# One 512-column product for two of 256, a ring of four banks for it, and a first stage fed by a transposed input

## The chip, the cores and the metric

The program runs on one core of a Trainium2 chip. The metric is the time of one execution on the device in microseconds (us). Engines are named as in the profile: PE is TensorE (PEld its loads of the stationary operand), DVE is VectorE, ACT is ScalarE, POOL is GpSimd, SP is SyncE, which issues the DMAs.

## The reference

Two layers over x of 256 tokens by 1024 features, all float32. Each layer is FFN, mixer, FFN; layer 0 mixes with a causal convolution, layer 1 with a gated recurrence (HGRN2). Every sub-layer normalizes its input and its output. Cut to what the change touches:

```python
def rms_norm(x, gain):
    y = x * lax.rsqrt(jnp.mean(x * x, axis=-1, keepdims=True) + EPS)
    return y * gain

def swiglu_ffn(x, w_in, w_out):                       # w_in 1024 x 5632, w_out 2816 x 1024
    gate, up = jnp.split(x @ w_in, 2, axis=-1)
    return (jax.nn.silu(gate) * up) @ w_out

for layer in range(2):
    h = swiglu_ffn(rms_norm(x, g[0]), ffn_w_in[layer, 0], ffn_w_out[layer, 0])
    x = x + 0.5 * rms_norm(h, g[1])
    x = x + rms_norm(mixer(rms_norm(x, g[2])), g[3])  # convolution or HGRN2
    h = swiglu_ffn(rms_norm(x, g[4]), ffn_w_in[layer, 1], ffn_w_out[layer, 1])
    x = x + 0.5 * rms_norm(h, g[5])
```

## The kernel before

Precision comes from splitting. Each float32 operand becomes a rounded high part and the rest (`split`: an ACT cast, then a DVE subtract), and each product is three products: high by high, high by low, low by high. Weights stream from HBM in pieces of 128 x 1024 (`weight`: one DMA of 512 KB from SP's queue into one of four `raw` buffers, then the split into one of ten `wh` and ten `wl` buffers). A chunk of an FFN is 256 hidden features: four pieces of the first matrix and two of the second; there are 11 chunks.

An FFN begins with `start`. For each of the two blocks of 128 tokens `pre_norm` transposes x by PE (8 transposes, two PSUM banks of the ring `tr`) and evacuates it with the gain, high part by ACT, low part by DVE, into `xth` and `xtl`; the row's mean square and its power of -0.5 (by POOL) follow beside it and are applied later as a scale of each token. For the first chunk `project` (in the very first FFN `project_both`) multiplies with the tokens as stationary operand and 512 columns of weights moving; `up` applies the scale and the gate, `turn` transposes the result. For the chunks 1 to 10 `up_both` computes both blocks at once with the hidden features as output rows: `channels` has the weights as stationary operand, and the 256 tokens move. It does two parts, the gate's rows and the up rows, each of 8 x 3 products of 256 columns into one half of an `mm` bank, and one DVE multiply of 512 columns (L286) takes both out of PSUM with the tokens' scales. Then come a sigmoid, two multiplies and a split. `down` multiplies chunk c-1 with the second matrix (`expand`, 512 columns) into two accumulator banks for each block. `post_norm` ends a sub-layer. The second block's end (`rest`) is run within the next sub-layer's `start`. HGRN uses `channels` eight times too, for its forget gates and queries.

PSUM has eight banks: four for the ring `acc` (the four accumulators of an FFN), two for `mm`, two for `tr`.

The text of the kernel is in program order. A planner puts the instructions of each engine in order by their readiness and priority; `tc.issue_after(ins)` pins what is traced in its block behind `ins` on that engine's queue. Before, the first weights' splits are pinned behind the first evacuations in this way. DMAs go through SP's queue in order; a weight's DMA waits there until its `raw` buffer is free.

The start: x is loaded in three DMAs, then the weights; PE transposes block 0, starts the projection, transposes block 1, and goes on.

Of the kernel before, what the change touches and what calls it, by code (L numbers as in the profile page):

```python
# [8 lines left out]
F32 = mybir.dt.float32  # L9
F32R = mybir.dt.float32r  # L10
# [30 lines left out]
def trunk_kernel(  # L41
    ctx: ExitStack,
    tc: tile.TileContext,
    x_in: bass.AP,
    wts: bass.AP,
# [28 lines left out]
    def narrow(tag, dtype=F32):  # L74
        return new(sb, [P, 256], dtype, tag, {"e": 4, "hid": 4}[tag])
# [7 lines left out]
    def mm():  # L83
        return new(ps, [P, 512], F32, "mm", 2)

    def tr():
        return new(ps, [P, 512], F32, "tr", 2)
# [11 lines left out]
    xth = const.tile([P, NT * D], F32R, name="xth")  # L99
    xtl = const.tile([P, NT * D], F32R, name="xtl")  # L100
    xkh = xth.rearrange("p (t k m) -> p k t m", t=NT, m=P)
    xkl = xtl.rearrange("p (t k m) -> p k t m", t=NT, m=P)
    gcol = const.tile([P, G_END], F32, name="gcol")
    nc.sync.dma_start(xs[0][:, :512], x_in[0, :P, :512])
    nc.sync.dma_start(gcol, cols)
    nc.sync.dma_start(xs[0][:, 512:], x_in[0, :P, 512:])
    nc.sync.dma_start(xs[1], x_in[0, P:, :])

    stream = [0]
    ahead = []  # L110
    last_hi = [None]
    last_split = [None]
    last_raw = [None]

    def weight(fine=False):
        n, half = divmod(stream[0], 2)
        stream[0] += 1
        src = new(sb, [P, 1024], F32, "raw", 4)
        last_raw[0] = nc.sync.dma_start(src, wts[n, :, half * 1024 : half * 1024 + 1024]).ins
# [3 lines left out]
        with ExitStack() as held:  # L123
            if stream[0] <= 4:
                held.enter_context(tc.issue_after(last_hi[0]))
            for a in range(0, 1024, step):
                split(hi[:, a : a + step], lo[:, a : a + step], src[:, a : a + step])
        return hi, lo

    def split(dst_h, dst_l, src):  # L130
        last_split[0] = act.copy(dst_h, src).ins  # L131
        dve.tensor_tensor(dst_l, src, dst_h.bitcast(F32), op=ALU.subtract)  # L132
# [28 lines left out]
    def pre_norm(t, gi):  # L161
        src = xs[t]
        hi, lo = xth[:, t * D : (t + 1) * D], xtl[:, t * D : (t + 1) * D]
        for h in range(2):
# [4 lines left out]
            for j in range(4):  # L169
                k = h * 4 + j  # L170
                g = gcol[:, gi * KD + k : gi * KD + k + 1]
                last_hi[0] = act.activation(hi[:, k * P : (k + 1) * P],
                                            pt[:, j * P : (j + 1) * P], AF.Copy, scale=g).ins
# [8 lines left out]
        if gi == 0:  # L182
            return hi, lo, None
        return hi, lo, mean_square(src)

# [35 lines left out]

    def project_both(xt, ws):
        o = [mm(), mm()]
# [619 lines left out]
```

## Time and profile before

| | |
|---|---|
| median of three timed runs | 1033.92 us (1032.2 to 1036.58) |
| the profiled execution's own time | 1030.74 us |
| its span | 1029.0 us |
| granted TensorE clock, mean | 0.996 |
| bytes moved by DMA | 181.14 MB, mean 176 GB/s |
| PE, PEld, DVE, ACT busy | 98%, 89%, 69%, 49% of the span |

All rows come from the profiled execution. Busy time is the time in which an engine had at least one instruction under way. Matmuls overlap, so a matmul's listed duration is longer than the time that it adds to a stream; the step from one start to the next shows the latter.

### The profile page before, as it was taken

The numbers are of one execution on the slowest core, as the hardware profiler recorded it, in microseconds if no ns is written. First come the engines' busy times: TensorE is split into PE (matmuls) and PEld (weight loads), VectorE is DVE, ScalarE is ACT, GpSimd is POOL, SyncE is SP. The second block draws the span as 40 slices with busy tenths as digits, with TensorE's granted clock in tenths as the row PEclk, the third lists the DMA queues.
The fourth block names the chain that finished last, engine by engine and source line by source line (L and its number), as shares of the span: only waits on it lengthen the run. The fifth ranks groups of instructions, "written<-read, shape, count | busy, mean of one in ns | idle before, by whom it ended". The sixth has DMA issues, their size and how long they took to land. (4 is left out here: it accounts for less than half of the span.)

```text
span 1029.0 us, 16850 instructions
## 1 busy us (share of the span) xinstructions
PE 1004.7 (98%) x6676; PEld 913.2 (89%) x6676; DVE 705.6 (69%) x1092; ACT 504.7 (49%) x852; POOL 71.0 (7%) x116
## 2 busy tenths in 40 slices
PE   7999999999899999999999999999999999999997
PEld 6999999888779999998899999989888879999996
DVE  6766666899887565658675656677676586666663
ACT  7544444764485444446544444574143473444441
POOL 1000000000010000000100000021343020000000
PEclk9999999999999999999999999999999999999999
DMA  7756464843536465647464646555222555564641
GB/s 254 259 198 212 156 211 142 270 164 111 182 101 226 168 199 170 223 152 241 144 206 163 205 164 226 185 202 179 87 84 91 176 175 186 161 215 155 215 143 41
DMA packets 50510, 181.14 MB, mean 176 GB/s; under 512 B 5985, under 2 KB 6113, under 8 KB 50432
## 3 DMA queue, kind: packets, MB, share of 16 engines
q1 hardware_dynamic: 50432, 180.07, 52.6%
q8 instruction: 52, 0.85, 0.3%
q14 instruction: 26, 0.21, 0.1%
HBM read 179.00 MB, written 1.05 MB: 175 GB/s over the span
## 5 line engine op out<-in xcount | busy, mean ns | idle before, releaser
L132 DVE TENSOR_TENSOR wl<-raw,wh 128x1024 fp32r<-128x1024 f32 (+1 forms) x386 | 400.6, 1059 | 200.4 <-ACT wh L131 196.8
L131 ACT CAST wh<-raw 128x1024 fp32r<-128x1024 f32 (+1 forms) x386 | 336.5, 923 | 275.4 <-PE mm L282 127.5
L281 PE MATMUL mm<-xth,wh 128*128 128x256 f32 x1408 | 396.3, 281 | 0.0
L282 PE MATMUL mm<-xtl,wh 128*128 128x256 f32 x1408 | 396.3, 281 | 0.0
L283 PE MATMUL mm<-xth,wl 128*128 128x256 f32 x1408 | 396.0, 281 | 0.0
L281 PEld LDWEIGHTS mm<-xth,wh 128*128 128x128 f32 x1408 | 265.8, 189 | 3.2 <-DVE e L335 0.7
L282 PEld LDWEIGHTS mm<-xtl,wh 128*128 128x128 f32 x1408 | 265.1, 188 | 2.6
L283 PEld LDWEIGHTS mm<-xth,wl 128*128 128x128 f32 x1408 | 266.1, 189 | 0.5 <-DVE wl L132 0.2
L136 PE MATMUL acc<-wl,b 128*128 128x512 f32 x352 | 137.8, 391 | 0.0
L137 PE MATMUL acc<-wh,b 128*128 128x512 f32 x352 | 137.7, 391 | 0.0
L135 PE MATMUL acc<-wh,b 128*128 128x512 f32 x352 | 137.6, 391 | 0.0
L137 PEld LDWEIGHTS acc<-wh,b 128*128 128x128 f32 x352 | 66.1, 188 | 14.1
L135 PEld LDWEIGHTS acc<-wh,b 128*128 128x128 f32 x352 | 66.1, 188 | 11.5
L136 PEld LDWEIGHTS acc<-wl,b 128*128 128x128 f32 x352 | 66.1, 188 | 11.4
L334 ACT ACTIVATE e<-ga 128x256 f32<-128x256 f32 x80 | 33.4, 418 | 79.8 <-DVE ga L286 79.8
L242 PE MATMUL mm<-wh,xth 128*128 128x512 f32 x176 | 70.7, 401 | 0.0
L243 PE MATMUL mm<-wl,xth 128*128 128x512 f32 x176 | 70.1, 398 | 0.0
L286 DVE TENSOR_TENSOR ga<-mm,scales 128x512 f32<-128x512 f32 x88 | 60.2, 685 | 12.4 <-PE mm L283 12.2
L146 POOL TENSOR_SCALAR tiny<-tiny 128x1 f32<-128x1 f32 (+1 forms) x30 | 8.4, 281 | 802.6 <-ACT b L212 711.5
L131 ACT CAST b<-e 128x256 fp32r<-128x256 f32 x80 | 32.4, 405 | 53.2 <-DVE e L336 53.2
L246 PE MATMUL mm<-wh,xtl 128*128 128x512 f32 x176 | 49.8, 397 | 0.0
L132 DVE TENSOR_TENSOR b<-e,b 128x256 fp32r<-128x256 f32 x80 | 33.8, 422 | 21.3 <-ACT b L131 21.3
(156 smaller groups left out, 877.4 us busy)
## 6 DMA issues: line engine op xcount, KB each, us to landing
raw<-wts SPq DMA_DIRECT2D x328, 512.0 KB, 5.0
b<-rows SPq DMA_DIRECT2D x10, 512.0 KB, 6.1
out_dram<-x SPq DMA_DIRECT2D x4, 256.0 KB, 2.1
x<-x_in SPq DMA_DIRECT2D x2, 256.0 KB, 2.8
x<-x_in SPq DMA_DIRECT2D x1, 512.0 KB, 4.2
b<-dft SPq DMA_DIRECT2D x1, 371.0 KB, 4.6
ca<-masks SPq DMA_DIRECT2D x1, 192.0 KB, 4.8
b<-w_dw SPq DMA_DIRECT2D x1, 124.0 KB
```

The lines of the kernel that those rows point to most:

```text
L131: last_split[0] = act.copy(dst_h, src).ins
L132: dve.tensor_tensor(dst_l, src, dst_h.bitcast(F32), op=ALU.subtract)
L135: pe.matmul(o, lh, rh, start=first, stop=False)
L136: pe.matmul(o, lh, rl, start=False, stop=False)
L137: pe.matmul(o, ll, rh, start=False, stop=last)
L242: pe.matmul(o, hi[:, kp], wh[:, sl], start=k == 0, stop=False)
L243: pe.matmul(o, hi[:, kp], wl[:, sl], start=False, stop=False)
L246: pe.matmul(o, a, w, start=False, stop=h == 1 and n == 3)
L281: pe.matmul(og, wh[:, cs], xkh[:, k], start=k == 0, stop=False)
L282: pe.matmul(og, wh[:, cs], xkl[:, k], start=False, stop=False)
L283: pe.matmul(og, wl[:, cs], xkh[:, k], start=False, stop=k == KD - 1)
L286: dve.tensor_tensor(pair(res), pair(o), scales.unsqueeze(1).broadcast_to([P, 2, SEQ]), op=ALU.mult)
```

## The change

- `channels`: for each k one product of 512 columns, weight high part by (x high, x low), and one of 256, weight low part by x high. Each part has a bank of its own: the first half collects high by high and low by high, the second half high by low. ACT copies the second half to SBUF, DVE adds it to the first, and a DVE multiply within SBUF applies the scales. For the moving operand high and low parts of x stand in one tile `xt` (block, part, k, token), with two small unused tiles on both sides of it that shift its address.
- PSUM: `mm` has four banks, and `tr` takes banks of `acc`'s four.
- The start: x is also handed over transposed, in four pieces of 256 features by 256 tokens. `boot` replaces `pre_norm` and `project_both` in the first FFN: for each piece it scales it into `xt`, loads and splits one weight, multiplies block 0, squares the piece, and multiplies block 1; the mean squares come from four small products with a column of ones. The order is pinned on ACT, DVE, PE and SP (`behind`). Twelve products of the identity with itself run before. The weights of chunk 1 are loaded before the second matrix's of chunk 0. The gains' DMA moves to ACT's queue.
- The plain x is loaded in chunk 4 of the first FFN, for the residual.
- The taps of the convolution get a row of zeros, and the ring `e` has six buffers where it had four.

```diff
@@ rings
-        return new(sb, [P, 256], dtype, tag, {"e": 4, "hid": 4}[tag])
+        return new(sb, [P, 256], dtype, tag, {"e": 6, "hid": 4}[tag])
-        return new(ps, [P, 512], F32, "mm", 2)
-
-    def tr():
-        return new(ps, [P, 512], F32, "tr", 2)
+        return new(ps, [P, 512], F32, "mm", 4)
+
+    tr = acc
...
-    xth = const.tile([P, NT * D], F32R, name="xth")
-    xtl = const.tile([P, NT * D], F32R, name="xtl")
-    xkh = xth.rearrange("p (t k m) -> p k t m", t=NT, m=P)
-    xkl = xtl.rearrange("p (t k m) -> p k t m", t=NT, m=P)
+    const.tile([P, 88], F32, name="before_xt")
+    xt_all = const.tile([P, NT * 2 * D], F32R, name="xt")
+    const.tile([P, 40], F32, name="after_xt")
+    xhl = xt_all.rearrange("p (t s k m) -> p k s t m", t=NT, s=2, m=P)
...
+    act.dma_start(gcol, cols)
...
+    def behind(*engines):
+        held = ExitStack()
+        for eng in engines:
+            last = next((i for i in reversed(nc.cur_bb.bb.instructions) if i.engine == eng.engine), None)
+            if last is not None:
+                held.enter_context(tc.issue_after(last))
+        return held
@@ boot
+    def boot():
...
+        for j in range(12):
+            sl = slice(j % 4 * P, (j % 4 + 1) * P)
+            pe.matmul(warm[:, sl], ident, ident, start=True, stop=True)
+
+        def bring(i):
+            src = part(pieces, i)
+            nc.sync.dma_start(src, x_turned[i])
+            for j in range(2):
+                k = 2 * i + j
+                g = gcol[:, k : k + 1]
+                xk = pair(src[:, j * SEQ : (j + 1) * SEQ])
+                act.activation(xhl[:, k, 0], xk, AF.Copy, scale=g)
+                dve.scalar_tensor_tensor(xhl[:, k, 1], xk, g, xhl[:, k, 0].bitcast(F32),
+                                         op0=ALU.mult, op1=ALU.subtract)
...
+        for i in range(4):
+            with behind(act, dve, pe, nc.sync):
+                bring(i)
+            with behind(act, dve, pe, nc.sync):
+                ws.append(weight(True))
+                multiply(0, i)
+            with behind(act, dve, pe):
+                act.activation(part(squares, i), part(pieces, i), AF.Square)
+                if i > 0:
+                    dve.tensor_tensor(total, total, part(squares, i), op=ALU.add)
+            if i == 3:
+                with behind(dve, pe):
...
+                    dve.tensor_scalar(ms, pt[:, :NT], 1.0 / D, EPS, op0=ALU.mult, op1=ALU.add)
+                    pool.tensor_tensor(r, ms, mhalf[:, :NT], op=ALU.pow)
+            with behind(pe):
+                multiply(1, i)
@@ channels
-        o = mm()
+        res = wide("ga")
         for part in range(2):
-            og = o[:, part * SEQ : (part + 1) * SEQ]
+            o = mm()
+            pair = o.rearrange("p (s t m) -> p s t m", s=2, m=P)
             for k in range(KD):
                 wh, wl = ws[k // 2]
                 col = (k % 2) * 512 + cols_[part]
                 cs = slice(col, col + P)
-                pe.matmul(og, wh[:, cs], xkh[:, k], start=k == 0, stop=False)
-                pe.matmul(og, wh[:, cs], xkl[:, k], start=False, stop=False)
-                pe.matmul(og, wl[:, cs], xkh[:, k], start=False, stop=k == KD - 1)
-        res = wide("ga")
-        pair = lambda ap: ap.rearrange("p (g n) -> p g n", g=2)
-        dve.tensor_tensor(pair(res), pair(o), scales.unsqueeze(1).broadcast_to([P, 2, SEQ]),
-                          op=ALU.mult)
+                pe.matmul(pair, wh[:, cs], xhl[:, k], start=k == 0, stop=False)
+                pe.matmul(pair[:, 0], wl[:, cs], xhl[:, k, 0], start=False, stop=k == KD - 1)
+            cross = narrow("e")
+            act.copy(cross, o[:, SEQ:])
+            dve.tensor_tensor(res[:, part * SEQ : (part + 1) * SEQ], o[:, :SEQ], cross, op=ALU.add)
+        grp = res.rearrange("p (g n) -> p g n", g=2)
+        dve.tensor_tensor(grp, grp, scales.unsqueeze(1).broadcast_to([P, 2, SEQ]), op=ALU.mult)
@@ ffn, first chunk of the first FFN
-        fetch(0)
-        o = project_both(xt, w1[0]) if extra is not None else [None, None]
-        up(0, 0, o[0])
-        up(1, 0, o[1])
+        if before is None:
+            stream[0] = 12
+            w1[1] = []
+            for n in range(4):
+                with behind(act, dve, nc.sync):
+                    w1[1].append(weight(True, 6 + n))
+                with behind(act, dve):
+                    if n < NT:
+                        up(n, 0, o[n])
+            with behind(act, dve, nc.sync):
+                w2[0] = [weight(True, 4 + n) for n in range(2)]
+            w2[1] = [weight(True, 10 + n) for n in range(2)]
+        else:
+            fetch(0)
+            for t in range(NT):
+                up(t, 0, None)
@@ constants
+        if c == 4:
+            with behind(nc.sync):
+                for t in range(NT):
+                    nc.sync.dma_start(xs[t], x_in[0, t * P : (t + 1) * P, :])
```

## Rows read from the trace of the kernel before

**Rows 1.** The page's table of busy time: time in us, share of the span, number of instructions.

```profile
PE 1004.7 (98%) x6676; PEld 913.2 (89%) x6676; DVE 705.6 (69%) x1092; ACT 504.7 (49%) x852; POOL 71.0 (7%) x116
```

**Rows 2.** Busy time by stage: the stage, its length, then PE, PEld, DVE, ACT and POOL busy (number of instructions), the granted clock, DMA's share, GB/s. The stages are the start, the rest of the first FFN, the second stretch of HGRN, and most of the last FFN.

```profile
0.00:24.00 24.00, 17.80 (x68) 13.85 (x69) 14.31 (x32) 17.64 (x44) 3.66 (x14) 1.00 0.75 259
24.00:204.00 180.00, 179.31 (x1259) 166.21 (x1258) 124.78 (x190) 92.58 (x144) 2.12 (x4) 1.00 0.63 205
...
755.00:826.00 71.00, 69.19 (x401) 58.13 (x401) 49.37 (x70) 25.69 (x39) 18.89 (x21) 1.00 0.39 126
...
848.00:1008.00 160.00, 160.00 (x1162) 151.69 (x1162) 98.65 (x134) 69.66 (x96) 2.06 (x2) 1.00 0.53 175
```

**Rows 3.** Groups of PE's instructions by line: `channels` (L281; L282 and L283 have as many) and `expand` by way of `mm3` (L135; L136 and L137 have as many): shapes, number, busy us, mean ns of one, idle before.

```profile
L281 PE MATMUL mm<-xth,wh 128*128 128x256 f32 x1408 | 396.3, 281 | 0.0
...
L135 PE MATMUL acc<-wh,b 128*128 128x512 f32 x352 | 137.6, 391 | 0.0
```

**Rows 4.** PE's timeline in a stretch of `channels`: start us, duration us; the first and the last of 16 starts.

```profile
60.16 0.28 PE L283 MATMUL mm<-xth,wl 128*128 128x256 f32 x1
...
61.94 0.28 PE L283 MATMUL mm<-xth,wl 128*128 128x256 f32 x1
```

**Rows 5.** The same in a stretch of `expand`: the first and the last of 11 starts.

```profile
64.20 0.40 PE L135 MATMUL acc<-wh,b 128*128 128x512 f32 x1
...
66.48 0.39 PE L136 MATMUL acc<-wl,b 128*128 128x512 f32 x1
```

**Rows 6.** The same in `project`: four products in one row, and the start of the next.

```profile
219.74 1.09 PE L246 MATMUL mm<-wh,xtl 128*128 128x512 f32 x4
220.67 0.39 PE L242 MATMUL mm<-wh,xth 128*128 128x512 f32 x1
```

**Rows 7.** The same in the convolution, whose stationary operand has 81 columns (128*81): the first and the last of 8 starts.

```profile
223.13 0.28 PE L135 MATMUL tr<-lg,b 128*81 128x256 f32 x1
...
223.96 0.28 PE L136 MATMUL tr<-lg,b 128*81 128x256 f32 x1
```

**Rows 8.** The same in HGRN's scores: 16 products of 64 columns in one row, and the start of the next.

```profile
719.26 1.97 PE L562 MATMUL tr<-b,b 128*128 128x64 f32 x16
721.04 0.37 PE L282 MATMUL mm<-xtl,wh 128*128 128x256 f32 x1
```

**Rows 9.** Groups of DVE's instructions by line and shape; columns as in the third group. `mm`, `acc` and `tr` are PSUM, the rest is SBUF.

```profile
L132 DVE TENSOR_TENSOR wl<-raw,wh 128x512 fp32r<-128x512 f32 x116 | 75.3, 683 | 9.6 <-ACT wh L131 7.1 <-PE mm L282 2.4
L286 DVE TENSOR_TENSOR ga<-mm,scales 128x512 f32<-128x512 f32 x88 | 60.2, 685 | 12.4 <-PE mm L283 12.2
...
L318 DVE SCALAR_TENSOR_TENSOR e<-mm,tiny,e 128x256 f32<-128x256 f32 x8 | 3.8, 477 | 1.5 <-ACT e L316 1.5
...
L132 DVE TENSOR_TENSOR hid<-tr,hid 128x256 fp32r<-128x256 f32 x8 | 3.3, 413 | 0.0
...
L213 DVE SCALAR_TENSOR_TENSOR b<-b,b 128x512 f32<-128x512 f32 x4 | 2.6, 682 | 0.0
```

**Rows 10.** The same for ACT: a copy of 256 columns out of PSUM.

```profile
L270 ACT COPY scales<-tr 128x256 f32<-128x256 f32 x5 | 1.9, 372 | 2.3 <-PE tr L268 2.3
```

**Rows 11.** The chain that ended last, in HGRN: start us, us, what.

```profile
752.18 0.60 DVE ga L286
...
754.16 1.03 DVE b L527
755.24 1.16 PE tr L547 x8
```

**Rows 12.** PE's timeline in the start: the projection's first product, two at the change of pace, and its last two.

```profile
9.52 0.80 PE L135 MATMUL mm<-wh,xth 128*128 128x512 f32 x1 [1.54 <-ACT wh L131]
...
13.96 0.63 PE L137 MATMUL mm<-wh,xtl 128*128 128x512 f32 x1
...
14.38 0.46 PE L135 MATMUL mm<-wh,xth 128*128 128x512 f32 x1
...
23.08 0.39 PE L136 MATMUL mm<-wl,xth 128*128 128x512 f32 x1
...
23.31 0.40 PE L137 MATMUL mm<-wh,xtl 128*128 128x512 f32 x1
```

**Rows 13.** The timeline of POOL and DVE in the start: a power of -0.5, and the first evacuation of `channels`.

```profile
17.78 1.00 POOL L148 TENSOR_TENSOR tiny<-tiny,mhalf 128x1 f32<-128x1 f32 x1
...
33.39 0.68 DVE L286 TENSOR_TENSOR ga<-mm,scales 128x512 f32<-128x512 f32 x1
```

**Rows 14.** Busy time in stretches of 2 us of the start; columns as in the second group. The last number is GB/s.

```profile
2.00:4.00 2.00, 0.62 (x3) 0.65 (x4) 0.00 (x0) 0.20 (x1) 0.00 (x0) 1.00 0.89 262
4.00:6.00 2.00, 1.59 (x7) 0.79 (x5) 0.32 (x2) 1.21 (x5) 0.00 (x0) 1.00 0.93 330
6.00:8.00 2.00, 1.12 (x4) 0.72 (x4) 1.70 (x8) 1.08 (x4) 0.00 (x0) 1.00 0.97 297
8.00:10.00 2.00, 0.48 (x1) 0.41 (x2) 0.73 (x2) 1.14 (x2) 0.00 (x0) 1.00 1.02 401
10.00:12.00 2.00, 2.00 (x8) 1.69 (x7) 2.00 (x4) 1.70 (x4) 0.00 (x0) 1.00 0.80 293
```

## Prediction: where the time goes, part by part

> **What bounds the kernel now.** First the page's table of busy time [rows 1]: the reader is to see that PE is busy 98% of the span, DVE 69%, ACT 49%. Then the same by stage [rows 2]: between 24 and 204 us PE is busy 179.3 of 180 us, and in the last FFN (848 to 1008 us) all of 160, so in the four FFNs every nanosecond that PE saves or loses is a nanosecond of the end. The exceptions are the start (17.8 of 24 us) and the mixers; the second HGRN stretch shows PE 69.2 of 71.
>
> Next the products themselves. A matmul's listed duration (281 ns for 256 columns [rows 3]) is not what it costs, because they overlap; the cost is the step from one start to the next, read off the timeline. In `channels`, 15 starts lie between 60.16 and 61.94 us [rows 4]: 1.78 / 15 = 119 ns for 256 columns. In `expand`, 10 starts between 64.20 and 66.48 [rows 5]: 228 ns for 512 columns. In `project`, four products between 219.74 and 220.67 [rows 6]: 233 ns. Two short products cost 237 ns, one long one 228 to 233: a short product carries more than half of a long one's cost.
>
> Is that surplus the load of the stationary operand? Two views say no. Short products whose load has 81 columns instead of 128 step by (223.96 − 223.13) / 7 = 119 ns too [rows 7]. And 16 products of only 64 columns, each with a 128-column load, take 1.78 / 16 = 111 ns [rows 8]: that is a load's own pace, below 119. So what a product costs is columns plus a fixed part: solving 119 and 228 gives 109 ns for 256 columns and 10 ns per product.
>
> **The joint product.** `channels` now does, for each k, one product of 512 columns (wh against hi and lo of x) and one of 256 (wl against hi), where three of 256 stood. The loop runs 8 times for each of 2 parts in 88 calls: 1408 triples [rows 3], of which 80 calls, 1280 triples, are in the FFNs and 128 in HGRN. Columns stay 768; one product and one load go. A triple costs 3 × 119 = 357 ns now.
>
> No row has 512 columns that move out of x, so the pair is bounded. The cheapest rows give 228 + 119 = 347; `project`'s 233 + 119 gives 352; a long product priced per column like the short one, 238 + 119, gives 357 and no gain. I take 347: the row nearest is `expand`'s, for in `project` x is what is loaded, and in the joint product, as in `expand`, it is not. The moving operand is now four runs of 128 elements; it is two runs in `channels` today and one run in [rows 7], both at 119 ns, so a break in the run shows no price. The third product adds to columns that the joint one has just written; today all three add to the same 256 columns in a row, which is no easier. Saving: 10 ns × 1280 = 13 us in the FFNs. In HGRN the 128 triples would give 1.3 us more; I don't count them, for the reason below. Bounds for the FFNs: 0 (pair at 357) to 19 us (342, if every product took a further 2 to 3 ns less, the change in x's place among the tiles included).
>
> **What the joint product puts on other engines.** Each part now needs an ACT copy of 256 columns out of PSUM (372 ns by the copy in [rows 10]), a DVE add of 256 with one side in PSUM (413 by the `hid` row of [rows 9]), and each call a DVE multiply of 512 within SBUF (682 by the 512-column `b<-b,b` row) instead of one from PSUM (685). That is 2 × 413 + 682 − 685 = 823 ns of DVE and 744 ns of ACT a call. In the stretch 24 to 204 us with its 20 calls: DVE 124.8 + 16.5 = 141 of about 178 us (79%), ACT 92.6 + 14.9 = 107 (60%) [rows 2]. Both stay below PE, so I cost them at nothing. The cover is distance: `hid` of chunk c is read by `down` one or more `up_both` later (5.6 us each), the ring of weights holds 10 pieces for the 6 of a chunk, and four own `mm` banks leave a call's two banks free for the whole next call. Without the cover, 160 times the 1.2 us of longer evacuation would be on the path.
>
> In HGRN the cover is thin. The chain that ended last runs through DVE there, the scaling in `channels` (L286) among it [rows 11]: forget gate, then query, then scores. An evacuation of 372 + 413 + 682 ns instead of 685 adds 0.8 us where PE has nothing else. I take 1.8 us lost for two such places, less 1.3 for the triples: 0.5 us lost (bounds −1.3 and +3).
>
> **Transposes in the ring of the accumulators.** `tr` now takes its bank from the ring of four `acc` banks. At a sub-layer's border the first token's accumulators are read by the post-norm before x is updated, and the transposes need that x, so their banks are free by then; the second token's two stay held and two are left. In the convolution four banks instead of two serve u and v. I cost it at nothing; bound ±3 us over the borders.
>
> **Loads.** x comes transposed, 1 MB, and once more plain, 1 MB, for the residual, at chunk 4. That second load stands in SP's queue among weights that run four buffers ahead, in a stretch with a DMA share of 0.63 [rows 2]; xs is read only after 200 us. Nothing; if uncovered, 1.05 MB at 300 GB/s, 3.5 us. The extra row of the taps is nothing likewise.
>
> **The start.** Today 16 transposes and 16 + 16 evacuations stand ahead of or between the first products; the first product starts at 9.52, products step by 0.43 us until 14.38 and by 0.23 after [rows 12]: half clock, though the stage's granted clock reads 1.00. The projection's last product starts at 23.31. From 14.38 PE does not pause, and at 33.3 it has done in addition the first `up_both` half and `down(0, 0)`: the first L286 starts at 33.39 [rows 13].
>
> After: no transposes, and four steps of (x piece 0.26 MB, weight 0.52 MB). At the rates of [rows 14] 0.58 MB is in by 4 us, 1.2 by 6, 1.8 by 8, 2.6 by 10, 3.2 by 12, so the weight of steps 0 to 3 (0.8, 1.6, 2.4, 3.2 MB with the gains' 0.03) lands near 4.8, 7.3, 9.5 and 12. DVE per step: 2 scalings (477 each), 2 half splits (683 each), one add (682): 3.0 us. It begins near 3.7 (first piece and an ACT scaling), waits about 1 us for the first weight, and ends its four steps near 15.5 [rows 9]. PE's 48 products of 0.23 are 11 us, and the last twelve wait for step 3: projection done near 17.5 to 18, some 5.5 us earlier than now.
>
> Then something else is late: the next weights. Their splits are queued by hand on ACT and DVE, the first ahead of `up` of token 0 and the second behind it. `up` waits for the norm (four small products, a DVE step, GpSimd's pow of 1.0 us [rows 13]), so it starts near 18.2. DVE then waits for the sigmoid (0.4), owes two `up` (4 × 477 ns) and three pieces (6 × 683) and finishes the fourth piece near 24.6; the first part of `up_both` can't end before that. Then 2.8 us for the second part and 2.7 for `down(0, 0)` give 30.3, against 33.3: 3 us gained. Bounds: 6 us if the splits don't hold PE, and 2 us lost if PE, waiting in bits between 18 and 24.6, falls back to half clock.
>
> **The sum.** 1030.7 (profiled execution, span 1029.0) − 13.2 − 3 + 0.5 = 1015. The three timed runs have a median of 1033.9, 3.2 above the profiled one, so I predict 1018.
>
> **The rivals.**
>
> *The long product costs per column what a short one does.* Then the pair is 357 and only the start pays: 1033.9 − 3 + 0.5 = 1031. For it: `project`'s 233 is half way there, and rows with 238 would not be far; against: the 1056 products of `expand` form the nearest rows, at 228. Chance 0.12. The Trainium skill (TensorE: Matmul & The Clock Gate, Back-to-back issue gap) gives a warm product N/2.4 + 2.5 ns, so one product less would save 2.5 ns; by that estimate 1280 times, 3.2 us, and a time near 1028. The trace disagrees on the constant: 119 ns at 256 columns where the page has 109.
>
> *The loads are the bound.* If the load sets the 119, the pair's second load hides under the long product, and the short one costs its columns and no more: 228 + 107 = 335, 22 ns × 1280 = 28 us, a time of 1003. Against it stand [rows 7] and [rows 8]. Chance 0.08. The Trainium skill (Perfetto Trace Analysis, Identifying the Most-Contended Engine) has headroom on TensorE judged by LDWEIGHTS busy time; here that is 89% [rows 1], which would make dropping a third of these loads a large gain.
>
> *The start gives nothing.* Product as forecast, but PE waits for the fourth piece at half clock: 1033.9 − 13.2 + 0.5 and 0 to 2 us, 1021 to 1023. For it: DVE sets the time after 18 us. Chance 0.17.
>
> *Slower: the four runs.* If each of the two further breaks in the moving operand cost 12 ns, the pair would be 371, 14 ns × 1280 = 18 us lost, a time of 1049. It decides from a long product of about 240 ns (no change) and 246 (slower by 0.5%). Against: two runs cost no more than one. Chance 0.05.
>
> My forecast has the remaining 0.58, with a range of its own of 1010 to 1025.
>
> **Range and chances.** A measurement of this kernel tells about 0.5% (5 us) from no change. The range runs from 1007 (between forecast's low end and the loads' case) to 1029 (short of the per-column case): outside stand most of the loads' 0.08 and the per-column and slower cases, partly. Faster: 0.58 + 0.08 + 0.17 = 0.83; same 0.12; slower 0.05.
>
> **What would show it.** In the trace after: the pair's two starts 347 ns apart and PE still busy above 98% from 30 to 200 us; DVE near 79% and ACT near 60% there; the first long products at 5 to 6 us, the projection's end near 18, DVE busy without a pause to about 25, and the first `down` done near 30. The prediction is wrong if the pair steps by 352 or more, if PE shows waits for ACT or DVE within the FFNs, or if the clock falls in the start.

## The result: 1047 us, 1.3% slower

The changed kernel takes 1046.97 us (median of four runs, 1045.13 to 1048.91) beside 1035.25 us for the kernel before: a ratio of 1.0127 (95% interval 1.0102 to 1.0153). The forecast was 1018 us, a gain. The profiled execution has a span of 1044.8 us, 15.8 more than before.

The table of busy time of the kernel after (it answers to [rows 1]):

```profile
PE 1004.2 (96%) x5284; PEld 848.8 (81%) x5284; DVE 772.4 (74%) x1264; ACT 557.3 (53%) x1016; POOL 70.0 (7%) x111
```

PE has 1392 instructions fewer and is busy for the same time. The first update of each block's x by `post_norm` (L218 before, L277 after) shows where the 15.8 us are. The stretches between these updates, in us:

| stretch ends with x of | before | after | rings | text3 | text4 |
|---|---|---|---|---|---|
| FFN 1, block 0 | 199.8 | 197.2 | 199.6 | 196.8 | 196.7 |
| FFN 1, block 1 | 7.7 | 9.9 | 7.7 | 11.3 | 10.6 |
| convolution, block 0 | 81.9 | 90.4 | 91.4 | 84.4 | 84.6 |
| convolution, block 1 | 11.7 | 19.5 | 19.8 | 12.4 | 12.3 |
| FFN 2, both | 189.1 | 186.1 | 187.0 | 187.3 | 187.5 |
| FFN 3, both | 189.0 | 187.8 | 189.5 | 187.6 | 187.4 |
| HGRN, block 0 | 145.4 | 146.0 | 146.9 | 152.8 | 146.3 |
| HGRN, block 1 | 13.8 | 18.9 | 17.6 | 13.5 | 13.9 |
| FFN 4, both | 186.2 | 184.5 | 185.7 | 185.4 | 185.4 |

(`rings`, `text3` and `text4` are experiments below. Each column is one execution, and executions of one kernel lie up to 5 us apart, 1032.2 to 1037.3 for the kernel before, so a difference of a microsecond in one cell decides nothing.) The FFNs' first stretches and FFN 2 to 4 gain 2.6 + 3.0 + 1.2 + 1.7 = 8.5 us. The mixers and the stretches in which one sub-layer passes into the next lose 2.2 + 8.5 + 7.8 + 0.6 + 5.1 = 24.2. Two of these terms are not what they seem. FFN 1's second block loses nothing in `rings`, where the products are the old ones, and 1.8 and 1.6 us in `after_old` and `joint_old`, where the transposes have their own ring: so most of the 2.2 are not the rings', and how they arise was not found. And 2.1 of FFN 2's 3.0 us are gained in `rings` too, without the joint product.

Busy time by stage of the kernel after (columns as in [rows 2], to whose first, second and last lines these answer; the third and fourth are the end of the convolution and the passage behind HGRN):

```profile
0.00:24.00 24.00, 20.95 (x104) 17.35 (x105) 15.17 (x30) 16.63 (x34) 3.94 (x11) 1.00 0.73 247
24.00:204.00 180.00, 178.66 (x933) 149.98 (x933) 138.43 (x231) 104.61 (x184) 0.89 (x2) 1.00 0.63 212
262.00:300.00 38.00, 22.25 (x97) 18.64 (x97) 24.63 (x52) 17.18 (x44) 2.56 (x6) 0.79 0.28 100
826.00:847.00 21.00, 18.36 (x82) 15.09 (x81) 11.79 (x25) 10.11 (x25) 3.49 (x7) 0.92 0.27 80
847.00:1009.00 162.00, 160.59 (x838) 136.47 (x837) 116.42 (x177) 85.89 (x145) 3.60 (x7) 1.00 0.58 193
```

The same two stretches of the kernel before:

```profile
262.00:300.00 38.00, 32.80 (x155) 26.08 (x154) 32.38 (x69) 26.18 (x67) 2.55 (x8) 0.96 0.39 132
826.00:847.00 21.00, 20.78 (x98) 16.78 (x97) 18.85 (x37) 16.94 (x41) 3.64 (x8) 1.00 0.59 200
```

From 262 to 300 us PE was busy 32.80 us and is now busy 22.25, at a mean granted clock of 0.79; DVE, ACT and DMA do less too. (The windows are equal in time, so they do not hold quite the same work.) No engine is loaded more, so the loss is waiting, not work. PE's timeline there, after (in brackets: idle time before, and what ended it):

```profile
266.53 0.39 PE L139 MATMUL acc<-cc,b 81*128 81x256 f32 x1 [4.32 <-ACT cc L135]
...
276.18 0.58 PE L139 MATMUL acc<-cc,b 81*128 81x256 f32 x1 [4.47 <-ACT cc L135]
...
281.35 1.97 PE L515 MATMUL acc<-ident,b 128*128 128x128 f32 x8 [2.77 <-DVE b L505]
282.97 0.78 PE L139 MATMUL acc<-wh,xt 128*128 128x512 f32 x1
...
298.41 1.94 PE L172 MATMUL acc<-ident,x 128*128 128x128 f32 x8 [3.67 <-DVE x L277]
300.00 0.78 PE L139 MATMUL acc<-wh,xt 128*128 128x512 f32 x1
300.58 0.63 PE L140 MATMUL acc<-wl,xt 128*128 128x512 f32 x1
```

And before:

```profile
270.93 0.40 PE L135 MATMUL acc<-wh,xth 128*128 128x512 f32 x1
...
276.06 0.28 PE L135 MATMUL tr<-cc,b 81*128 81x256 f32 x1
...
281.81 1.11 PE L454 MATMUL tr<-ident,b 128*128 128x128 f32 x8 [0.21 <-DVE b L444]
...
290.25 0.66 PE L168 MATMUL tr<-ident,x 128*128 128x128 f32 x4 [0.48 <-DVE x L218]
290.67 0.47 PE L135 MATMUL acc<-wh,xth 128*128 128x512 f32 x1
```

Before, the 48 products of the convolution's output for block 0 start at 270.93 and fill PE until the late inputs come: the last inverse transform (`cc`, 276.06), the transposes of block 1 (L454, 281.81) and of the next pre-norm (L168, 290.25) wait 0.5 us at most. (Only the inverse transform ahead of them waited, 2.77 us at 265.35; it is the 4.32 of after.) After, the same products (L139, 282.97) stand behind block 1's transposes (L515), and those of block 1 (300.00) behind the pre-norm's (L172). The transposes wait for their inputs, ready products stand behind them, and after each pause the first products step by 0.42 us and more (300.00 to 300.58), the lower of the two clock levels (1.2 GHz), where 0.23 is the full pace.

### The profile page after: what moved, and what is told of

Read it like the earlier page. It is cut to its first block, busy times and chain, and to the rows that moved or that the text cites. A ratio compares the mean times of both kernels' runs of the same rounds, so it can differ in the third digit from the quotient of the medians.

```text
span 1044.8 us, 14556 instructions
## 1 busy us (share of the span) xinstructions
PE 1004.2 (96%) x5284; PEld 848.8 (81%) x5284; DVE 772.4 (74%) x1264; ACT 557.3 (53%) x1016; POOL 70.0 (7%) x111
## 5 line engine op out<-in xcount | busy, mean ns | idle before, releaser
L330 PE MATMUL mm<-xt,wh 128*128 128x512 f32 x1408 | 501.7, 399 | 0.3 <-ACT wh L135 0.3
L136 DVE TENSOR_TENSOR wl<-raw,wh 128x1024 fp32r<-128x1024 f32 (+1 forms) x386 | 401.7, 1061 | 75.0 <-ACT wh L135 73.5
L135 ACT CAST wh<-raw 128x1024 fp32r<-128x1024 f32 (+1 forms) x386 | 341.7, 922 | 113.2 <-DMA raw<-wts 61.7
L331 PE MATMUL mm<-xt,wl 128*128 128x256 f32 x1408 | 395.0, 281 | 0.0
L330 PEld LDWEIGHTS mm<-xt,wh 128*128 128x128 f32 x1408 | 264.3, 188 | 64.4 <-DVE ga L336 0.7
L331 PEld LDWEIGHTS mm<-xt,wl 128*128 128x128 f32 x1408 | 265.8, 189 | 3.4 <-DVE wl L136 0.3
L139 PE MATMUL acc<-wh,b 128*128 128x512 f32 x352 | 138.2, 393 | 0.0
L333 ACT COPY e<-mm 128x256 f32<-128x256 f32 x176 | 64.8, 369 | 125.2 <-PE mm L331 120.0
L334 DVE TENSOR_TENSOR ga<-mm,e 128x256 f32<-128x256 f32 x176 | 72.2, 420 | 73.4 <-ACT e L333 73.0
L139 PEld LDWEIGHTS acc<-wh,b 128*128 128x128 f32 x352 | 66.4, 189 | 14.9 <-ACT b L135 0.2
L290 PE MATMUL mm<-wh,xt 128*128 128x512 f32 x176 | 70.1, 399 | 0.5 <-DVE ga L334 0.5
L291 PE MATMUL mm<-wl,xt 128*128 128x512 f32 x176 | 70.2, 399 | 0.0
L336 DVE TENSOR_TENSOR ga<-ga,scales 128x512 f32<-128x512 f32 x88 | 60.9, 692 | 1.3
L135 ACT CAST b<-e 128x256 fp32r<-128x256 f32 x80 | 32.5, 407 | 40.6 <-DVE e L385 40.6
L384 DVE TENSOR_TENSOR e<-e,ga 128x256 f32<-128x256 f32 x80 | 33.8, 423 | 22.3 <-ACT e L383 22.3
L294 PE MATMUL mm<-wh,xt 128*128 128x512 f32 x176 | 50.2, 399 | 0.0
```

The costliest lines, as they stand in the source:

```text
L139: pe.matmul(o, lh, rh, start=first, stop=False)
L290: pe.matmul(o, hi[:, kp], wh[:, sl], start=k == 0, stop=False)
L291: pe.matmul(o, hi[:, kp], wl[:, sl], start=False, stop=False)
L330: pe.matmul(pair, wh[:, cs], xhl[:, k], start=k == 0, stop=False)
L331: pe.matmul(pair[:, 0], wl[:, cs], xhl[:, k, 0], start=False, stop=k == KD - 1)
L333: act.copy(cross, o[:, SEQ:])
```

## The experiments

Each ran beside the kernel before; ratios are to it. A correction first: in `micro` and `sweep` I first averaged the pairs over one long step too many. The pairs that later expectations quote from them (353, 349.5) are about 3 ns too high; the numbers below are over whole pairs.

### rings and share: only the transposes' ring

```diff
     def mm():
-        return new(ps, [P, 512], F32, "mm", 2)
+        return new(ps, [P, 512], F32, "mm", 4)      # share: 2, as before
-    def tr():
-        return new(ps, [P, 512], F32, "tr", 2)
+    tr = acc
...
-            o = tr()        # taps' spectrum
+            o = mm()
```

> The kernel before with the PSUM rings of the change alone: four mm banks, transposes from acc's four (the taps' spectrum from mm). Theory 1, the transposes' share of acc's ring holds expand back (convolution's end, the borders convolution to FFN and HGRN to FFN): those stages lose the 20 to 24 us that they lose in the changed kernel, 1055 to 1059 us. Theory 2, four mm banks let the gates of the convolution run ahead and leave its tail uncovered: about 1043 to 1050, with the loss in the convolution alone. Theory 3, the joint product's extra DVE and ACT work or the new start is behind the loss: no change, 1033 to 1037.

> The kernel before with the transposes taken from acc's ring, and mm left at two banks. Theory 1: the same loss as with both edits, 1053 to 1059 us. Theory 2: no loss, 1033 to 1038. Theory 3: no change.

Measured: `rings` 1051.72 us, ratio 1.019 (1.0175 to 1.0205); `share` 1054.09, ratio 1.0218 (1.0199 to 1.0237). The old products and the old start, with the rings alone changed, lose more than the whole change does, in the convolution and behind both mixers (table; `share` takes 91.9, 20.5 and 18.7 us there). The time of `rings` lies between the ranges of theories 1 and 2; that the loss is not in the convolution alone decides for theory 1. PE's timeline of `rings`:

```profile
282.11 1.97 PE L453 MATMUL acc<-ident,b 128*128 128x128 f32 x8 [3.90 <-DVE b L443]
283.73 0.78 PE L134 MATMUL acc<-wh,xth 128*128 128x512 f32 x1
...
299.56 1.94 PE L167 MATMUL acc<-ident,x 128*128 128x128 f32 x8 [3.67 <-DVE x L217]
301.16 0.78 PE L134 MATMUL acc<-wh,xth 128*128 128x512 f32 x1
```

The same order, and waits of 3.90 and 3.67 us where the change has 2.77 and 3.67. With two `mm` banks the loss is there too, so four `mm` banks are not its cause; sharing is. (Both also move the taps' spectrum, a few products in FFN 1, to `mm`.) The Trainium skill (Perfetto Trace Analysis, Optimization Strategy) reads a repeated gap on the engine that should be saturated as a possible sign of too few buffers. The number is a rival here, for the six banks of `acc` and `tr` became four, and a shared ring of six was not run. The trace speaks against it. DVE's last reads of the convolution's u and v in the changed kernel:

```profile
273.60 0.41 DVE L484 TENSOR_TENSOR cb<-acc,b 81x256 f32<-81x256 f32 x1
...
278.61 0.43 DVE L495 TENSOR_TENSOR b<-acc,b 128x256 f32<-128x256 f32 x1 [0.32 <-PE acc L141]
```

In the text of the kernel u and v are four banks ahead of the two accumulators, so by that order theirs are the banks that the products take. They were read out at 274.01 and 279.04, and the products' inputs were split by 278.3 (L136). Yet the products start at 282.97, behind the transposes whose input came at 281.35.

### after_fix: the transposes in mm's ring instead

```diff
+    tm = mm
...
-            pt = tr()        # pre_norm, transposed, turn of the convolution
+            pt = tm()
```

> The changed kernel with the transposes of pre_norm, of the convolution's turn and of transposed taken from mm's ring; only scores, the token scales and the convolution's u and v stay in acc's. Theory 1: the mixers' loss goes, the gains of the start and the FFNs stay, about 1026 us (1022 to 1031). Theory 2: the convolution still loses its 8 us, 1034 or more. Theory 3: no better than the changed kernel, 1045.

Measured: 1067.6 us, ratio 1.0331 (1.0303 to 1.0359): a miss, and worse than the change itself. The two passages that I meant to mend did mend (13.1 and 13.7 us, from 19.5 and 18.9). But FFN 1's second block took 11.0, HGRN 156.9, and each of FFN 2 to 4 some 6 us more. PE's timeline behind FFN 1:

```profile
202.52 0.40 PE L142 MATMUL acc<-wh,b 128*128 128x512 f32 x1
210.27 1.94 PE L173 MATMUL mm<-ident,x 128*128 128x128 f32 x8 [7.35 <-issue]
211.86 0.78 PE L291 MATMUL mm<-wh,xt 128*128 128x512 f32 x1
```

Now the second pre-norm's transposes (L173), in `mm`, stand ahead of the next projection (L291), which takes the next `mm` bank and had its input. The wait went to whichever ring the transposes share. The miss gave the theory its present form: a ring hands out its banks in the order of the text, so an instruction with a late input holds up everything that is written after it in the same ring, however ready.

### after_text, text3, text4: another order of the text, and late steps in the other ring

If that is the mechanism, another order of the text must give time back with the rings as they are. `after_text` puts the ready products ahead of the late transposes:

```diff
     def start(gi, before):
-        first = pre_norm(0, gi)
         before()
+        first = pre_norm(0, gi)
...
-        sbt = turn(1, norm(1))
+        zb = norm(1)
         accs = [acc(), acc()]
         expand(accs, blocks(*sa, KD), wo, True, True)
+        sbt = turn(1, zb)
```

> The changed kernel with its rings and products untouched; only the order of the program text differs at the borders: the last products of a sub-layer's second block (rest) stand ahead of the next sub-layer's first pre-norm, and in the convolution the products of the first block (expand t0) stand ahead of the transposes of the second (turn(1)). Theory (a ring gives its banks out in the order of the text, so a late transposition holds up the ready products written after it): the waits of 2.77 us ahead of turn(1)'s transposes and of 3.67 us ahead of the pre-norm's, with the half clock behind them, go; but the chain behind each of these transposes (4 to 5 us of evacuation) then has no products above it. So part comes back: 1039 to 1044, the convolution near 87 us and the two borders near 17, the FFNs as they were. Rival (the loss comes from the longer evacuation of the joint product or from the fifth and sixth e buffer, not from the order): 1045 to 1049.

Measured: 1049.07 us, ratio 1.0161 (1.0146 to 1.0176). A miss: it lies at the rival's upper end. The waits ahead of the transposes went, as expected (the two passages take 14.6 and 14.0 us), but the waits behind them grew, and the convolution's first block took 96.6 us where some 87 were expected. PE's timeline:

```profile
204.26 0.50 PE L290 MATMUL mm<-wh,xt 128*128 128x512 f32 x1 [2.97 <-ACT xt L176]
...
269.19 0.58 PE L139 MATMUL acc<-cc,b 81*128 81x256 f32 x1 [6.45 <-ACT cc L135]
...
280.14 0.58 PE L139 MATMUL acc<-cc,b 81*128 81x256 f32 x1 [5.96 <-ACT cc L135]
...
298.61 0.50 PE L139 MATMUL acc<-wh,xt 128*128 128x512 f32 x1 [2.69 <-ACT xt L135]
...
314.32 0.80 PE L290 MATMUL mm<-wh,xt 128*128 128x512 f32 x1 [3.24 <-ACT xt L176]
```

The steps that PE waits for there (the evacuation of a transposition, L176, and splits, L135) have no products above them any more. This run alone doesn't tell the theory from its rival. `text3` interleaves instead: half of the ready products, the transposes, the other half. It also lets three late steps draw from `mm`: the convolution's turn, its last `conv(1, 3)` and HGRN's transposes.

```diff
     def start(gi, before):
+        finish = before()            # first half of rest's products
         first = pre_norm(0, gi)
-        before()
+        finish()                     # second half, and post_norm
...
-        pt = tr()                    # transposed
+        pt = tr() if gain is None else mm()
...
-                pt = tr()            # turn of the convolution
+                pt = mm()
...
+        both = [[acc(), acc()], [acc(), acc()]]
+        expand(both[0], blocks(*sa, KD)[:4], wo[:4], True, False)
+        conv(1, 3, mm)
+        expand(both[0], blocks(*sa, KD)[4:], wo[4:], False, True)
         sbt = turn(1, norm(1))
```

> The changed kernel with the text interleaved: half of rest's products, then the pre-norm's transposes of the first block, then the other half; in the convolution half of expand t0, then the last conv(1, 3), then the other half, then turn(1). turn, the last conv(1, 3) and HGRN's last transposes take banks of mm, which are idle there and whose next users are late too. All products of the change stay. Theory: every late transposition now has ready products ahead of it in the text and products after it, so nearly all of the 24 us comes back: the convolution 82 to 85 us (90.4 in the changed kernel), the border behind it 11 to 14 (19.5), the border behind HGRN 13 to 15 (18.9), FFNs within 1 us of the changed kernel; 1024 to 1030 in all. Rival (the joint product itself, or four mm banks, costs the mixers their time): over 1040.

Measured: 1040.51 us, ratio 1.0073 (1.0057 to 1.0089). In the sum a miss (1024 to 1030 expected, and the rival over 1040), but convolution and both passages are where the theory put them (84.4, 12.4, 13.5 us): 18.5 us back. HGRN took 152.8 us instead of 146.0. PE's timeline in its scores, `text3`:

```profile
779.39 1.97 PE L633 MATMUL acc<-b,b 128*128 128x64 f32 x16 [0.51 <-DVE b L644]
783.28 2.83 PE L633 MATMUL acc<-b,b 128*128 128x64 f32 x16 [1.91 <-DVE b L644]
788.01 1.94 PE L633 MATMUL acc<-b,b 128*64 128x64 f32 x16 [1.89 <-DVE b L644]
```

Between the scores, where projections used to fill PE, stands nothing. I had put HGRN's first transposes into `mm`, ahead of those projections: the mechanism once more. `text4` undoes this alone.

```diff
     def transposed(src, hi, lo, n, base, gain=None):
-        pt = tr() if gain is None else mm()
+        pt = tr() if base == 0 else mm()
```

> As text3, but HGRN's transposes of the first four heads take their bank from acc again, as in the changed kernel; those of the last four stay in mm. In text3 these first transposes, whose input comes late, stood in mm's ring ahead of the projections of the second value half and of the gates, which had filled PE's time between the scores (the stretch from the end of FFN 3 to HGRN's first x update took 151.8 us, 145.0 in the changed kernel, with waits of 1.9 to 2.3 us ahead of the scores). Theory: that stretch goes back to 144.5 to 146.5, the projections stand between the scores again, and the time to 1033 to 1036; the rest stays as in text3. Rival (the interleaved text itself costs HGRN the time, whatever ring the transposes use): 150 to 152 and about 1040.

Measured: 1032.63 us (ten runs), ratio 0.9998 (0.9984 to 1.0012); HGRN 146.3 us. The projections are back between the scores:

```profile
782.79 1.97 PE L633 MATMUL acc<-b,b 128*128 128x64 f32 x16 [0.25 <-DVE b L644]
784.57 1.18 PE L294 MATMUL mm<-wh,xt 128*128 128x512 f32 x4
785.59 0.39 PE L290 MATMUL mm<-wh,xt 128*128 128x512 f32 x1
...
786.67 1.11 PE L633 MATMUL acc<-b,b 128*64 128x64 f32 x16 [0.23 <-DVE b L644]
```

With the change's products, start and two rings of four all kept, the order of the text, and which of the two rings a late step draws from, take the ratio from 1.0127 to 0.9998: some 13 us, all of the change's loss. How much of it is the order and how much the ring was not separated, except in HGRN, where `text4` differs from `text3` in one line; the interleaved text on the old rings was not run either. Of the 24 us, 3.0 stay lost from FFN 1 to the convolution and 2.6 in the convolution; what would fill those waits was not tried.

### after_old, joint_old, start_only: the parts on the old rings

`after_old` is the changed kernel with 2 `mm` and 2 `tr` banks; `joint_old` is the kernel before with the joint product, x's new place and the six `e` buffers only; `start_only` has the new start only.

```diff
# after_old (the taps' spectrum also goes back to tr)
-        return new(ps, [P, 512], F32, "mm", 4)
+        return new(ps, [P, 512], F32, "mm", 2)
-    tr = acc
+    def tr():
+        return new(ps, [P, 512], F32, "tr", 2)
```

> The changed kernel with the PSUM rings of before: four acc, two mm, two tr (the joint product's two parts take mm's two banks in turn). Theory 1, a ring hands out its banks in the order of the text, and transposes that wait for late input hold back the products that would fill the time: with their own ring the mixers and borders take what they took before, and what is left is the joint product (1408 x 5.0 ns = 7.0 us), project's 528 x 5 ns = 2.6 us and the start's 2.6 us: 1020 to 1025 against a before of 1032 to 1034. Rival: two mm banks don't do for the joint product, each part waits for the evacuation of the one before the last, 0.3 to 1 us in 176 parts: 1040 or more.

> The joint product alone (with x in one tile between its two small tiles, and six e buffers), on the rings of before and with the start of before. Theory 1: 7.0 + 2.6 us gained, 1022 to 1025 against 1032 to 1034, pair 352 to 353 ns. Rival, two mm banks don't do: 1040 or more.

> The start alone: the kernel before with the transposed input in four steps, its old channels, its old place of x and its old rings. First post-norm about 2.6 us earlier than before as in the changed kernel, the rest as before: 1030 to 1031 against 1032 to 1034. Rival, the start's other order of weights and the plain x's load cost later what it gives: no change.

Measured: `after_old` 1029.78 us, ratio 0.9971 (0.9959 to 0.9982); `joint_old` 1031.52, 0.999 (0.9978 to 1.0001); `start_only` 1029.96, 0.9975 (0.9965 to 0.9985). `start_only` is where it was expected; the other two are misses, some 5 and 7 us above the range of theory 1 and far below the rival's. With their own ring the transposes' stretches are what they were: in `after_old` the convolution takes 83.0 and 11.6 us and the passage behind HGRN 13.8, where the change takes 90.4, 19.5 and 18.9 and the kernel before 81.9, 11.7 and 13.8. The start alone shortens FFN 1's first stretch from 199.8 to 197.5 us. The joint product alone gains 1.0 to 1.2 us in each of FFN 2 to 4, and loses 3.1 in FFN 1, 1.6 behind it and 1.3 in HGRN: on the old rings it brings nothing on top of the start. PE's timeline of `joint_old` there:

```profile
51.09 0.50 PE L139 MATMUL acc<-wh,b 128*128 128x512 f32 x1 [2.60 <-ACT b L135]
51.43 0.40 PE L140 MATMUL acc<-wl,b 128*128 128x512 f32 x1
```

`down` waits for the split of `hid` (L135): with two `mm` banks the longer evacuation does come through, once. In `after_old`, with two banks as well, PE waits 2.34 us for `hid` at 29.87 and 1.5 more in two places up to 49.62; with four banks it waits 1.19 there and not again before 198 us. So two banks cost the joint product some of its gain, four leave none to the transposes, and the two pull against each other. No version beats the kernel before by 0.5%; the two best gain 0.3%.

### micro and sweep: what a pair costs by itself

Both compute nothing of the reference: streams of products on fixed data, 24 pairs or triples of each form.

```diff
# sweep; micro has a stream like this for each of its forms
+    def pairs(b, off, loff):
+        for n in range(N):
+            c = col(n % 6)
+            l = slice(c.start + loff, c.stop + loff)
+            a = n % 4 * 512 + off
+            mm(banks[b], wh[:, l], xt[:, a : a + 512], n == 0, False)
+            mm(banks[b][:, :SEQ], wl[:, l], xt[:, a : a + 256], False, n == N - 1)
```

> A bench of streams of products alone; nothing of the reference is computed. Steps between starts. Theory A, each product costs its columns and 10 ns: a pair 347 ns in every form, 512 columns 228, 256 columns 119. Theory B, four runs in the moving operand cost 7 to 9 ns: pairs with contiguous columns 347, with four runs 354, and 512 columns alone 236 against 228. Theory C, the alternation costs it, since the load for the long product (111 ns) runs under a short one of 107 ns of columns: pairs 354 with four runs and with contiguous columns alike, 512 columns alone 228 in both forms, pairs with loads of 64 columns 347 or less, and eight long ones followed by eight short ones 347 a pair. Theory D, the bank: pairs whose two products go to two banks 347, to one bank 354.

> The bench of streams again; nothing of the reference is computed. Pairs of 512 and 256 columns, with the moving operand shifted by 0 to 416 bytes in ten cases, the loaded one by 32 to 416 bytes in seven, then triples of 256 in five. If place in SBUF is what lets 512 columns step by 228 in one stream and 233 to 236 in another, the pair moves between 342 and 357 with the shift; if not, all cases give 353.

Measured in `micro`, ns: a triple of 256 columns 360, with one run or two; a pair 350, with one run or four, in one bank or two; 512 columns alone 233, one load repeated or not; eight long, then eight short 354 a pair. Loads of 64 columns give 350 for the triple, 230 for the long product and 351 for the pair. None of the four theories has all of this. So neither runs nor banks cost anything here, a smaller load helps the triple and not the pair, and the pair saves 10. In `sweep` the operands are shifted in SBUF (elements of 4 bytes; moving operand, loaded operand):

| shift | 0, 0 | 16, 0 | 32, 0 | 96, 0 | 0, 16 | 0, 24 | 0, 64 | 0, 104 |
|---|---|---|---|---|---|---|---|---|
| pair | 350 | 347 | 353 | 353 | 347 | 353 | 350 | 353 |
| triple | 360 | | 355 | 355 | | 360 | | 353 |

The rows for a pair at 0, 0 (first two), at 16, 0 (next two), and for triples at 0, 0 and at 0, 104:

```profile
22.94 0.39 PE L45 MATMUL bank<-xt,wh 128*128 128x512 f32 x1
...
26.79 0.39 PE L45 MATMUL bank<-xt,wh 128*128 128x512 f32 x1
...
40.10 0.39 PE L45 MATMUL bank<-xt,wh 128*128 128x512 f32 x1
...
43.91 0.39 PE L45 MATMUL bank<-xt,wh 128*128 128x512 f32 x1
...
165.72 5.44 PE L45 MATMUL bank<-xt,wh 128*128 128x256 f32 x44
...
199.76 5.46 PE L45 MATMUL bank<-xt,wh 128*128 128x256 f32 x45
```

Eleven pairs in 3.85 us are 350 ns each, in 3.81 us 346; 43 steps in 5.44 − 0.28 us are 120 ns, 44 in 5.46 − 0.28 are 118. One product less is worth 10 ns at one place and nothing at another.

### text3_place: x's place in the kernel

```diff
-    const.tile([P, 88], F32, name="before_xt")
+    const.tile([P, 104], F32, name="before_xt")
...
-    const.tile([P, 40], F32, name="after_xt")
+    const.tile([P, 24], F32, name="after_xt")
```

> As text3, but xt begins 16 elements (64 bytes) later in each partition: the unused tiles on its two sides have 104 and 24 elements where they had 88 and 40. In the sweep a moving operand 16 elements further took 349.5 ns a pair where the changed kernel's place takes 353. If that holds here: the pair 349 to 350 ns, 3.2 ns x 1408 = 4.5 us less than text3, about 1 us in each FFN. Rival (the place counts only together with those of the weights, which stand at other addresses than in the sweep): the pair anywhere from 349 to 357 and the time within 5 us of text3, up or down.

Measured: 1038.51 us, ratio 1.0069 (1.0049 to 1.0089), not to be told from `text3`. The mean steps at full pace say more: the pair 349.7 ns (352.3 in the other), but `project`, which loads x, 233.3 ns (228.2). FFN 2 to 4 gain 0.6 to 0.9 us each; the convolution, where x enters by `project` alone, gives 1.1 back. The place counts in the kernel too, and not for all users alike.

## Point by point

**PE bounds the kernel.** Right in the FFNs (178.66 of 180 us busy, 160.59 of 162), and that is why the 24 us came from elsewhere: the forecast priced what PE does and took its order as given.

**A pair costs 347, 13.2 us saved.** Wrong in size. In the kernel after, the first pair and the end of the sixth in a row (answering to [rows 4, 5]):

```profile
59.88 0.40 PE L330 MATMUL mm<-xt,wh 128*128 128x512 f32 x1
60.11 0.28 PE L331 MATMUL mm<-xt,wl 128*128 128x256 f32 x1
...
62.00 0.40 PE L139 MATMUL acc<-wh,b 128*128 128x512 f32 x1
```

2.12 / 6 = 353 ns. Over all steps at full pace the mean is 352.3 (1293 uninterrupted pairs), and 355.9 for the triple before (1304; the forecast's 3 x 119 = 357 was a little high too). 3.5 ns x 1280 = 4.5 us, a third of the forecast; the pair lies at 352, which the prediction had named as the sign of being wrong. `project`, from x's new place, steps by 228.2 ns where it took 233.4. The term that was mis-sized: "10 ns per product" was solved from two streams (L281 and L135) whose operands lie at different places, and the place alone moves 768 columns by 7 ns. The per-column rival was nearer than its 0.12. The Trainium skill (TensorE: Matmul & The Clock Gate, Back-to-back issue gap) would, by its formula for an isolated product, have one product less save 2.5 ns: by that estimate 3.2 us. The kernel shows 3.5 ns, the streams by themselves 0 to 10.

**Other engines: nothing.** Right for the FFNs with four `mm` banks. After, the groups of ACT and DVE in `channels` (columns as in [rows 9]):

```profile
L334 DVE TENSOR_TENSOR ga<-mm,e 128x256 f32<-128x256 f32 x176 | 72.2, 420 | 73.4 <-ACT e L333 73.0
...
L333 ACT COPY e<-mm 128x256 f32<-128x256 f32 x176 | 64.8, 369 | 125.2 <-PE mm L331 120.0 <-issue 5.0
L336 DVE TENSOR_TENSOR ga<-ga,scales 128x512 f32<-128x512 f32 x88 | 60.9, 692 | 1.3
```

420, 369 and 692 ns were forecast as 413, 372 and 682; DVE is busy 138.43 us and ACT 104.61 in the stretch forecast at 141 and 107, and HGRN lost 0.6 us for 0.5. That last agreement is partly luck: `rings` loses 1.5 there without the joint product, `joint_old` 1.3 with it. The cover that I named, four `mm` banks, is what holds: with two, the wait of 2.60 us appears.

**Transposes in the accumulators' ring: nothing, at most 3 us.** This is the step that failed. It put the term at nothing because a bank is *free* when the transposes come ("their banks are free by then"), and it was. It did not ask who stands *behind* them in the ring. With a ring of their own, the transposes could come late and let the ready products pass; in one ring they can't. The convolution and the two passages behind the mixers lost 8.5 + 7.8 + 5.1 = 21.4 us; `rings`, with the old products, has a span 20.5 us longer than before (1049.5 and 1029.0). The bound that I gave was 3. With FFN 1's 2.2, HGRN's 0.6 and the pair's missing 8.7 us, less the 2.7 that `project` gained (5.2 ns x 528), that is some 30 of the 31.5 us between the forecast's span (1029.0 - 15.7 = 1013.3) and the measured one.

**Loads: nothing.** Right: no wait of PE near the load of plain x.

**The start: 3 us.** Right in size: 2.4 alone, and FFN 1's first stretch is 2.6 shorter in the change, some of the joint product's gain included. PE's timeline in the start, after (answering to [rows 12]):

```profile
6.67 0.49 PE L139 MATMUL acc<-wh,xt 128*128 128x512 f32 x1 [0.83 <-ACT wh L135]
...
19.48 0.39 PE L141 MATMUL acc<-wh,xt 128*128 128x512 f32 x1
...
30.29 0.50 PE L141 MATMUL acc<-wh,hid 128*128 128x512 f32 x1 [1.19 <-DVE hid L136]
```

The first product came at 6.67 us (forecast 5 to 6) and the projection's last at 19.48 (18), 3.8 us before the old one instead of 5.5. Of these a third is lost again: PE waits 1.19 us for the split of `hid`, which stands on DVE behind those of the next weights.

**The rivals.** The one that ended slower, the four runs, has the sign and not the cause: runs cost nothing (`micro`). That the loads bind fell: the pair gained 3.5 ns of 356, not 22. PEld went from 89% to 81% of the span, which by the Trainium skill (Perfetto Trace Analysis, Identifying the Most-Contended Engine) is headroom won; no time beyond the pair's gain came of it. That the start gives nothing fell as well. A wait at the borders I had only as a bound of 3 us, and it should have been the rival on the other side: who is behind the transposes was to be read from the diff and the timeline ([rows 1 to 14] hold no row of a border).

## What to carry over

When two rings of buffers are merged, list their users in program order and ask of each whether its input can be late; whatever is written behind a late one waits, even with free banks. Late and ready work keep separate rings, which here was the better way (`after_old`). Or the text is interleaved and late steps are spread over the rings, so that ready work stands both ahead of a late step and behind it (`text4`, no better than the kernel before). A price of some nanoseconds solved from streams at different addresses is no price; it needs the same operands at the same place.

## What the runs showed of the hardware

The step of a matmul stream moves with the place of its operands in SBUF: the same pair takes 347 to 353 ns, the same triple 353 to 360, by shifts of 32 to 416 bytes. Behind a wait PE falls to the lower clock level for a while: its instructions step at half pace from 298.41 to 301.42 us behind the wait of 3.67 (granted clock 0.50), and in `joint_old` from 51.90 to 55.04 behind that of 2.60 (0.51). So a wait costs more than its length, and the granted clock of the convolution's end (262 to 300 us) fell from 0.96 to 0.79.
